# Three row-tile pairs per product through seven block products of sums, in an fp32 encoder trunk

## The chip, the core and the metric

One core of a Trainium2 chip runs the whole program. The metric is device time in microseconds (us) of one execution. The kernel before was run three times: median 2261.09 us, from 2259.49 to 2262.24 us. A separate profiled execution took 2260.93 us, of which 2259.0 us lie between its first and its last instruction (the span).

## What is computed

Two layers of an encoder on 256 tokens with 2048 features, in fp32. Layer 0 mixes tokens by a neighbourhood attention, layer 1 by a short gated convolution; each is followed by a gated MLP of inner width 5632 with a convolution of three taps. Cut to what matters here:

```python
def short_conv_mixer(x, w_in, conv_w, w_out):
    gb, gc, h = jnp.split(x @ w_in, 3, axis=-1)
    return (gb * dwconv_centered(gc * h, conv_w)) @ w_out

def conv_glu_ffn(x, w_up, conv_w, conv_b, w_down):
    h = dwconv_centered(x @ w_up, conv_w) + conv_b
    g, u = jnp.split(h, 2, axis=-1)
    return (jax.nn.silu(g) * u) @ w_down

for i in range(DEPTH):                       # DEPTH = 2
    h = h + mixer(rms_norm(h, mix_norm[i]))  # 0: attention, 1: short convolution
    h = h + conv_glu_ffn(rms_norm(h, ffn_norm[i]), ...)
return rms_norm(h, final_norm)
```

The products `@ w_down` and `@ w_out` of the short convolution are what the change touches.

## The kernel before, in words

**Two kinds of product stage.** A `Phase` (lines 108 to 131) computes features by tokens: for each feature tile of 128 it runs over the K tiles, and each K tile takes two matmuls, line 130 with 512 columns (the weight's high part against the high and low part of the activations side by side) and line 131 with 256 columns (the weight's low part against the high part). A `Tokens` stage (lines 236 to 263) computes tokens by features: the activations are the stationary operand, a block of 512 weight columns the moving one, and the result is to be added to the residual stream `h`, which lies in SBUF as 2 token tiles by 2048 features. For each K tile and each of the two token tiles it runs three matmuls of 512 columns: high by high (line 259), high by low (260), low by high (261). Splitting each fp32 operand into a high and a low part of the faster type keeps the accuracy.

**Tokens stages.** There are six: the attention's output product (16 K tiles), two halves of the down projection in each layer (22 K tiles each) and the short convolution's output (16 K tiles). In each, four column groups g of 512 features are done one after another, each with two PSUM banks of the ring `mm` (four banks); when a group is through, `residual` (line 209) adds both banks to `h`. Where a norm follows (`to_norm`), the group's squares are summed on ScalarE (line 213), and one chunk later its four feature tiles are transposed on TensorE (line 221) and scaled and split into the next stage's input tiles `a` (lines 159 and 160). A Phase behind a norm begins with the first eight K tiles of three feature tiles (`intro=3`), so that input tiles 8 to 15 are needed only from its fourth chunk on. After the last group the norm's factor is worked out (`token_rstd`, lines 224 to 234). `last_evac` does the same for the end of the program and writes the output.

**Weights.** They come in chunks of 128 by 1024 values (512 KB), in a Tokens stage two K tiles of one column group. `prep_to` (lines 89 to 106) issues the chunk's DMA on the SP queue into a tile of the ring `raw` (5 tiles), casts it to its high part on ScalarE (line 97 or 104) and subtracts for the low part on VectorE (98 or 105), into rings `hi` and `lo` of 6 tiles each.

**Order.** The list `items` holds the chunks in the order in which TensorE consumes them. The main loop at the end of `trunk` calls, for each item, `prep_to(c + 1 + AHEAD)` with AHEAD = 4, then the item's `run`, then whatever `after(n, fn)` has put off by n items. This gives the order of priority; the framework that builds the program sets the order of each engine's queue from it and from what is ready in its own reckoning, so an instruction can stand a little earlier or later than it was written. Each queue is served in its order.

**Evacuations around it.** `up_evac` (419 to 436) and `sc_evac` (399 to 414) turn the PSUM results of a Phase into the K tiles `act[...]` and `yT[...]` that the Tokens stage after it reads, on ScalarE and VectorE; `split` (lines 155 and 156) makes their high and low parts. GpSimd has nothing to do in these stages.

Of the kernel before, what the change touches and what calls it, by code (L numbers as in the profile page):

```python
# [12 lines left out]
F32 = mybir.dt.float32  # L14
# [20 lines left out]


# [10 lines left out]
def trunk(ctx, tc, xT, par, bias, wqk, wv, wo, wsc, wscout, wup, wdown, out):  # L47
# [13 lines left out]
    NPAD = 5  # L61
# [27 lines left out]
    def prep_to(n):  # L89
        while len(prepped) < min(n, len(chunks)):  # L90
            src, w, kinds = chunks[len(prepped)]
            raw = wp.tile([P, CH * P], F32, name="raw", tag="raw", bufs=5)
            hi = wp.tile([P, CH * P], F32R, name="hi", tag="hi", bufs=6)
            lo = wp.tile([P, CH * P], F32R, name="lo", tag="lo", bufs=6)
            if kinds == 1:
                nc.sync.dma_start(out=raw[:, :w], in_=src)
                nc.scalar.copy(out=hi[:, :w], in_=raw[:, :w])  # L97
                nc.vector.tensor_sub(out=lo[:, :w], in0=raw[:, :w], in1=hi[:, :w].bitcast(F32))  # L98
            else:

                nc.sync.dma_start(out=raw.rearrange("p (f c) -> p f c", f=4), in_=src.rearrange("f p c -> p f c"))
                r = raw.rearrange("p (f k c) -> p f k c", f=4, c=P)
                hv, lv = (x.rearrange("p (k f c) -> p f k c", f=4, c=P) for x in (hi, lo))
                nc.scalar.copy(out=hv, in_=r)  # L104
                nc.vector.tensor_sub(out=lv, in0=r, in1=hv.bitcast(F32))  # L105
            prepped.append((hi, lo))

    class Phase:
# [3 lines left out]
        def __init__(self, w, fts, nk, src, evac, intro=0, step=CH):  # L112
# [4 lines left out]
            for ft, k0, n in order:  # L117
                k1 = min(k0 + n, nk)
                items.append((self, ft, len(chunks), k0, k0, k1))
                chunks.append((w[ft, :, k0 * P:k1 * P], (k1 - k0) * P, 1))  # L120

        def run(self, ft, c, k0, ka, kb):
            hi, lo = prepped[c]
# [82 lines left out]
    def residual(g, ps):  # L206
        for t in range(2):
            x = h[:, t, g * 4 * P:(g + 1) * 4 * P]
            nc.vector.tensor_add(out=x, in0=ps[t], in1=x)

    def squares(g, ssq):
        for t in range(2):
            nc.scalar.activation(tp.tile([P, 4 * P], F32, name="s", tag="s"), h[:, t, g * 4 * P:(g + 1) * 4 * P],
                                 AF.Square, accum_out=ssq[:, t, g:g + 1])
# [21 lines left out]
    class Tokens:  # L236


        def __init__(self, parts, src, evac):

            self.src, self.evac = src, evac
            self.nk = sum(n for _, n in parts)
            for g in range(KT // 4):
                for i, (w, n) in enumerate(parts):
                    base = sum(m for _, m in parts[:i])
                    for k0 in range(0, n, 2):
                        items.append((self, g, len(chunks), base + k0, base + k0, base + k0 + 2))
                        chunks.append((w[4 * g:4 * g + 4, :, k0 * P:(k0 + 2) * P], 8 * P, 2))

        def run(self, g, c, k0, ka, kb):  # L250
            hi, lo = prepped[c]
            if ka == 0:
                self.ps = [pm.tile([P, 4 * P], F32, name="mm", tag="mm") for _ in range(2)]
            for k in range(ka, kb):
                x = self.src[k]
                wh, wl = (w[:, (k - k0) * 4 * P:(k - k0 + 1) * 4 * P] for w in (hi, lo))
                for t in range(2):
                    xh, xl = (x[:, i + t * P:i + (t + 1) * P] for i in (0, S))
                    nc.tensor.matmul(self.ps[t], lhsT=xh, rhs=wh, start=k == 0, stop=False)  # L259
                    nc.tensor.matmul(self.ps[t], lhsT=xh, rhs=wl, start=False, stop=False)  # L260
                    nc.tensor.matmul(self.ps[t], lhsT=xl, rhs=wh, start=False, stop=k == self.nk - 1)  # L261
            if kb == self.nk:
                self.evac(g, self.ps)

    def to_norm(n, a):
# [3 lines left out]
        def evac(g, ps):  # L269
            residual(g, ps)  # L270
            squares(g, ssq)

            def next_input():
                for k0, tag in ((4 * g, "tr"), (4 * g + 2, "o")):
# [4 lines left out]
            after(1, next_input)  # L279
            if g == KT // 4 - 1:  # L280
                after(2, lambda: nc.vector.tensor_copy(rstd, token_rstd(ssq)))
# [11 lines left out]
    def qk_evac(f, ps):  # L293
# [4 lines left out]
        x["qk"[which]] = tp.tile([P, 2 * S], F32R, name=f"qk{which}", tag=f"qk{which}")  # L298
# [62 lines left out]
    class Values:  # L361


        def __init__(self, g, src):
            self.g, self.src = g, src
            for k0 in range(0, KT, 2):
                items.append((self, g, len(chunks), k0, k0, k0 + 2))
                chunks.append((wv[g, :, k0 * 4 * P:(k0 + 2) * 4 * P], 8 * P, 1))

        def run(self, g, c, k0, ka, kb):  # L370
            hi, lo = prepped[c]
# [13 lines left out]
            for t in range(2):  # L385
                vh = tp.tile([P, 4 * P], F32R, name=f"vh{t}", tag=f"vh{t}", bufs=1)
                vl = tp.tile([P, 4 * P], F32R, name=f"vl{t}", tag=f"vl{t}", bufs=1)
# [8 lines left out]
    yT = [None] * KT  # L396
    sc_of = {}

    def sc_evac(f, ps):
# [11 lines left out]
        else:  # L411
            nc.vector.tensor_mul(out=t, in0=t, in1=sc_of["c"])
            yT[j] = act_tile()
            split(yT[j], t)

# [3 lines left out]
    def up_evac(layer, act):  # L419
        def evac(f, ps):  # L420
# [11 lines left out]
            else:  # L432
                nc.vector.tensor_mul(out=c, in0=c, in1=glu["g"])
                act[j % HALF] = act_tile()
                split(act[j % HALF], c)
        return evac


    def last_evac():
# [3 lines left out]
        def evac(g, ps):  # L443
            residual(g, ps)
            squares(g, ssq)

            def outputs():
                for k0, tag in ((4 * g, "tr"), (4 * g + 2, "o")):
                    tr = transposed(k0, tag)
                    y[k0 // 2] = a_tile().bitcast(F32)  # L450
                    for k in range(2):
                        nc.scalar.activation(y[k0 // 2][:, k * S:(k + 1) * S], tr[:, k, :], AF.Copy,
# [147 lines left out]
```

## Time and profile before

| what | value |
|---|---|
| median of three runs | 2261.09 us |
| profiled execution | 2260.93 us |
| its span | 2259.0 us |
| TensorE matmul, busy | 2235.0 us (99%), 11908 instructions |
| weight load, busy | 1914.8 us (85%) |
| VectorE, busy | 1559.8 us (69%) |
| ScalarE, busy | 1158.4 us (51%) |
| mean granted TensorE clock | 0.997 of full speed |

Busy time is the time in which at least one instruction of the engine was under way. Instructions of one engine overlap a little, so a group's mean duration is longer than the step from one instruction to the next; the step is read from a timeline. For TensorE above all, a matmul's duration is about twice the time by which it moves the end.

### The profile page before, as it was taken

How to read it: one execution, taken by the hardware profiler on the slowest of the kernel's cores; microseconds unless marked ns; L12 is line 12 of the kernel's file. 1: busy time of each engine (PE TensorE's matmuls, PEld its weight loads, DVE VectorE, ACT ScalarE, POOL GpSimd, SP SyncE). 2: the span in 40 equal slices, each digit the busy share in tenths (PEclk: the TensorE clock that was granted, in tenths of full speed). 3: DMA queues.
4: the chain of work that ended last, by engine and by line, in shares of the span. 5: the costliest groups of instructions: out<-in, count | busy, mean ns of one | idle time of the engine just before them, and what ended most of it. 6: DMA issues, size and time to landing. Idle time of an engine off the chain costs nothing.

```text
span 2259.0 us, 31368 instructions
## 1 busy us (share of the span) xinstructions
PE 2235.0 (99%) x11908; PEld 1914.8 (85%) x11908; DVE 1559.8 (69%) x2263; ACT 1158.4 (51%) x1745; POOL 46.7 (2%) x52
## 2 busy tenths in 40 slices
PE   8999999999999999999999999999999999999997
PEld 6888888888888888888888888888888888888886
DVE  7777665688874577776567676558888547777643
ACT  5555545555553455554444444446555435555542
POOL 3110000000000000000000000000000000000000
PEclk9999999999999999999999999999999999999999
DMA  7565555555566655566655555555556665555662
GB/s 239 177 187 176 180 172 189 182 194 187 190 190 192 194 186 187 187 186 187 189 187 192 188 193 188 188 185 188 192 189 188 195 193 189 186 187 187 186 187 93
DMA packets 209687, 420.97 MB, mean 186 GB/s; under 512 B 13312, under 2 KB 136192, under 8 KB 209536
## 3 DMA queue, kind: packets, MB, share of 16 engines
q1 hardware_dynamic: 207792, 414.72, 58.6%
q0 software_dynamic: 1024, 3.15, 0.5%
q8 instruction: 94, 1.54, 0.3%
q10 hardware_dynamic: 720, 1.09, 0.1%
q14 instruction: 57, 0.47, 0.1%
HBM read 416.81 MB, written 2.10 MB: 185 GB/s over the span
## 4 chain that ended last, share of the span: by engine, by line
PE 98%; DVE 1%; issue 0%; ACT 0%; DVEq 0%; ACTq 0%
PE mm L130 42%; PE mm L131 21%; PE mm L261 10%; PE mm L259 10%; PE mm L260 10%; PE mm L379 1%; PE mm L380 1%; PE mm L381 1%; PE tr L221 1%; PE tr L341 0%; DVE a L464 0%; PE o L355 0%; PE o L353 0%; PE sc L316 0%; PE o L354 0%
## 5 line engine op out<-in xcount | busy, mean ns | idle before, releaser
L130 PE MATMUL mm<-a,hi 128*128 128x512 f32 x4096 | 1438.1, 397 | 6.0 <-DVE a L160 4.2
L131 PE MATMUL mm<-a,lo 128*128 128x256 f32 x4096 | 1142.3, 279 | 1.0 <-DVE lo L98 1.0
L130 PEld LDWEIGHTS mm<-a,hi 128*128 128x128 f32 x4096 | 769.2, 188 | 190.8 <-DVE a L160 6.0
L97 ACT CAST hi<-raw 128x1024 fp32r<-128x1024 f32 (+1 forms) x550 | 572.3, 1041 | 652.7 <-issue 516.9
L98 DVE TENSOR_TENSOR lo<-raw,hi 128x1024 fp32r<-128x1024 f32 (+1 forms) x550 | 672.7, 1224 | 335.0 <-ACT hi L97 334.5
L131 PEld LDWEIGHTS mm<-a,lo 128*128 128x128 f32 x4096 | 771.7, 188 | 2.9 <-DVE lo L98 1.9
L105 DVE TENSOR_TENSOR lo<-raw,hi 128x1024 fp32r<-128x1024 f32 x240 | 294.1, 1225 | 286.5 <-ACT hi L104 285.9
L104 ACT CAST hi<-raw 128x1024 fp32r<-128x1024 f32 x240 | 252.8, 1053 | 341.3 <-PE mm L261 266.9
L259 PE MATMUL mm<-hi,act 128*128 128x512 f32 x960 | 374.6, 390 | 0.0
L261 PE MATMUL mm<-hi,act 128*128 128x512 f32 x960 | 373.7, 389 | 0.0
L260 PE MATMUL mm<-lo,act 128*128 128x512 f32 x960 | 373.6, 389 | 0.0
L261 PEld LDWEIGHTS mm<-hi,act 128*128 128x128 f32 x960 | 180.2, 188 | 37.5
L259 PEld LDWEIGHTS mm<-hi,act 128*128 128x128 f32 x960 | 180.2, 188 | 37.0
L260 PEld LDWEIGHTS mm<-lo,act 128*128 128x128 f32 x960 | 180.2, 188 | 36.9
L184 DVE SCALAR_TENSOR_TENSOR conv<-pad,pt,conv 128x256 f32<-128x256 f32 x384 | 185.1, 482 | 8.6 <-ACT conv L182 2.0
L173 DVE TENSOR_TENSOR corr<-mm,corr 128x256 f32<-128x256 f32 x256 | 106.7, 417 | 0.0
L182 ACT ACTIVATE conv<-pad,pt 128x256 f32<-128x256 f32 x176 | 105.2, 598 | 0.8 <-DVE pad L174 0.8
L172 ACT COPY corr<-mm 128x256 f32<-128x256 f32 x256 | 92.7, 363 | 0.1
L174 DVE TENSOR_TENSOR pad<-corr,rstd 128x256 f32<-128x256 f32 x176 | 75.1, 427 | 5.8
L379 PE MATMUL mm<-hi,a 128*128 128x512 f32 x128 | 50.7, 396 | 0.0
L380 PE MATMUL mm<-lo,a 128*128 128x512 f32 x128 | 49.9, 390 | 0.0
L381 PE MATMUL mm<-hi,a 128*128 128x512 f32 x128 | 49.9, 390 | 0.0
(98 smaller groups left out, 793.8 us busy)
## 6 DMA issues: line engine op xcount, KB each, us to landing
raw<-in_wup SPq DMA_DIRECT2D x352, 512.0 KB, 3.6
raw<-in_wdown SPq DMA_DIRECT2D x176, 512.0 KB, 3.8
raw<-in_wsc SPq DMA_DIRECT2D x96, 512.0 KB, 3.6
raw<-in_wqk SPq DMA_DIRECT2D x58, 512.0 KB, 3.8
raw<-in_wv SPq DMA_DIRECT2D x32, 512.0 KB, 4.1
raw<-in_wo SPq DMA_DIRECT2D x32, 512.0 KB, 3.5
raw<-in_wscout SPq DMA_DIRECT2D x32, 512.0 KB, 3.6
raw<-in_wqk SPq DMA_DIRECT2D x12, 256.0 KB, 5.1
```

The source lines that it names most:

```text
L97: nc.scalar.copy(out=hi[:, :w], in_=raw[:, :w])
L98: nc.vector.tensor_sub(out=lo[:, :w], in0=raw[:, :w], in1=hi[:, :w].bitcast(F32))
L104: nc.scalar.copy(out=hv, in_=r)
L105: nc.vector.tensor_sub(out=lv, in0=r, in1=hv.bitcast(F32))
L130: nc.tensor.matmul(ps, lhsT=hi[:, o:o + P], rhs=x, start=k == 0, stop=False)
L131: nc.tensor.matmul(ps[:, S:], lhsT=lo[:, o:o + P], rhs=x[:, :S], start=False, stop=k == self.nk - 1)
L173: nc.vector.tensor_add(out=corr, in0=ps[:, :S], in1=corr)
L182: nc.scalar.activation(c, x[:, 1:S + 1], AF.Identity, scale=w[1], bias=b)
L184: nc.vector.scalar_tensor_tensor(out=c, in0=x[:, tap:tap + S], scalar=w[tap], in1=c, op0=ALU.mult, op1=ALU.add)
L259: nc.tensor.matmul(self.ps[t], lhsT=xh, rhs=wh, start=k == 0, stop=False)
L260: nc.tensor.matmul(self.ps[t], lhsT=xh, rhs=wl, start=False, stop=False)
L261: nc.tensor.matmul(self.ps[t], lhsT=xl, rhs=wh, start=False, stop=k == self.nk - 1)
```

## The change

A pair of K tiles and a pair of column groups form a product of 2 by 2 blocks: two token tiles by two K tiles, times two K tiles by two column groups of 512. Written out it has eight block products. The change computes it, for some pairs, with the scheme of seven block products of sums and differences (Winograd's form of Strassen's algorithm). The pairs are numbers 2, 5 and 8 of the eleven of each down stage (`S_DOWN`), and 1, 3 and 5 of the eight of the short convolution's output (`S_OUT`). The attention's output product has none, but goes through the new loop too.

- A Tokens stage now takes two column groups at a time (g runs over two, not four), with all four `mm` banks, named 11, 21, 12, 22. An item is still one chunk (left or right column group), and both halves of a plain pair are separate items. A pair of the set is one item, `seven`.
- Weights of such a pair: `sums` makes two tiles of sums on VectorE (four additions of 128 by 512), one in the ring `raw`, one in a tile `t24`. Three splits follow for the right chunk, where there was one: half of the raw chunk, and both sums. The left chunk is split as before.
- Activations: `make_forms`, called from the evacuations of the stage before, makes four sums of 128 by 128 on GpSimd, and splits them with one ScalarE copy and one VectorE subtraction of 128 by 512.
- Products: four of the seven accumulate in the PSUM banks of the pool `pa` (`st`, `sc`, `tr`, `o`), three go straight into 11, 12 and 21. One item after the last pair of the set, `combine` adds the four banks to `h`: one ScalarE copy, eight VectorE additions of 128 by 512.
- `residual` and `squares` work on one token tile and column group at a time. Norm inputs are made from two column groups at once (8 feature tiles, four transposing steps on four banks). At the end of the program half of the output scalings move from ScalarE to VectorE.
- To make room, `NPAD` goes from 5 to 3, and a few temporary tiles share tags (`vv`, `qk`).

```diff
+S_DOWN = (2, 5, 8)
+S_OUT = (1, 3, 5)
...
-    NPAD = 5
+    NPAD = 3
...
+            if kind == "cols":
+                prepped.append(parts(r) + (raw,))
             else:
...
+                prepped.append(sums(prepped[-1][2].rearrange("p (f k c) -> p f k c", f=4, c=P), r))
...
+    def sums(l, r):
+
+        t13 = wp.tile([P, CH * P], F32, name="raw", tag="raw", bufs=5)
+        t24 = tp.tile([P, CH * P], F32, name="t24", tag="qk")
+        v13, v24 = (x.rearrange("p (k f c) -> p f k c", f=4, c=P) for x in (t13, t24))
+        add = nc.vector.tensor_add
+        add(out=v13[:, :, 0, :], in0=l[:, :, 0, :], in1=r[:, :, 0, :])
+        add(out=v13[:, :, 1, :], in0=r[:, :, 1, :], in1=r[:, :, 0, :])
+        add(out=v24[:, :, 0, :], in0=v13[:, :, 0, :], in1=r[:, :, 1, :])
+        add(out=v24[:, :, 1, :], in0=v24[:, :, 0, :], in1=l[:, :, 1, :])
+        return parts(r[:, :, 1:2, :]), parts(t13), parts(t24)
...
-            for g in range(KT // 4):
...
+            for g in range(KT // 8):
+                base = 0
+                for w, n in parts:
                     for k0 in range(0, n, 2):
...
+                        k = base + k0
+                        left, right = (w[f:f + 4, :, k0 * P:(k0 + 2) * P] for f in (8 * g, 8 * g + 4))
+                        c = len(chunks)
+                        chunks.append((left, 8 * P, "cols"))
+                        if k // 2 in sset:
+                            chunks.append((right, 8 * P, "sums"))
+                            items.append((self, g, c + 1, k, k, k + 2))
+                        else:
+                            chunks.append((right, 8 * P, "cols"))
+                            items.append((self, g, c, k, k, k + 2))
+                            items.append((self, g, c + 1, k, k, k + 2))
+                    base += n
...
+    def seven(self, g, c, k0):
...
+        if first:
+            self.u = [pa.tile([P, 4 * P], F32, name="mu", tag=n) for n in ("st", "sc", "tr", "o")]
+        a, e, f, b = self.u
+        left, (w22, t13, t24) = prepped[c - 1], prepped[c]
...
+        for ps, x, w, j in ((a, raw(0, 0), left, 0), (self.c["11"], raw(1, 0), left, 1), (self.c["12"], s4, w22, 0),
+                            (e, s1, t13, 0), (f, s3, t13, 1), (b, s2, t24, 0), (self.c["21"], raw(1, 1), t24, 1)):
+            own = ps in self.u
+            self.product(ps, *x, *(y[:, j * 4 * P:(j + 1) * 4 * P] for y in w[:2]), own and first, own and last)
+        if last:
+            after(1, lambda: self.combine(g))
...
+    def combine(self, g):
+
+        a, e, f, b = self.u
+        sa, u = (tp.tile([P, 4 * P], F32, name="s", tag="s") for _ in range(2))
+        o = {(t, n): h[:, t, (2 * g + n) * 4 * P:(2 * g + n + 1) * 4 * P] for t in range(2) for n in range(2)}
+        nc.scalar.copy(out=sa, in_=a)
+        nc.vector.tensor_add(out=u, in0=b, in1=sa)
+        nc.vector.tensor_add(out=o[0, 0], in0=o[0, 0], in1=sa)
+        nc.vector.tensor_sub(out=sa, in0=e, in1=u)
+        nc.vector.tensor_sub(out=o[1, 1], in0=o[1, 1], in1=f)
+        nc.vector.tensor_add(out=u, in0=f, in1=u)
+        nc.vector.tensor_add(out=o[0, 1], in0=o[0, 1], in1=sa)
+        nc.vector.tensor_add(out=o[1, 1], in0=o[1, 1], in1=sa)
+        nc.vector.tensor_add(out=o[1, 0], in0=o[1, 0], in1=u)
...
+    def make_forms(xe, xo):
...
+        nc.gpsimd.tensor_sub(out=v[:, 0, :], in0=x21, in1=x22)
+        nc.gpsimd.tensor_sub(out=v[:, 1, :], in0=v[:, 0, :], in1=x11)
+        nc.gpsimd.tensor_add(out=v[:, 2, :], in0=x12, in1=v[:, 1, :])
+        nc.gpsimd.tensor_sub(out=v[:, 3, :], in0=x11, in1=x21)
+        v = v.rearrange("p f c -> p (f c)")
+        nc.scalar.copy(out=y[:, :4 * P], in_=v)
+        nc.vector.tensor_sub(out=y[:, 4 * P:], in0=v, in1=y[:, :4 * P].bitcast(F32))
+        return y
...
+                for k0, tag in zip(range(4 * q - 4, 4 * q + 4, 2), ("tr", "o", "sc", "st")):
...
+            if t and q % 2:
+                after(1, next_input)
...
+            Tokens([(wdown[layer, half], HALF)], act, evac if half else residual, S_DOWN, forms)
...
+    Tokens([(wscout, KT)], yT, to_norm(3, a3), S_OUT, yforms)
```

## Rows read from the trace of the kernel before

**Rows 1.** The page: engines' busy time; the last chain by engine.

```profile
PE 2235.0 (99%) x11908; PEld 1914.8 (85%) x11908; DVE 1559.8 (69%) x2263; ACT 1158.4 (51%) x1745; POOL 46.7 (2%) x52
...
PE 98%; DVE 1%; issue 0%; ACT 0%; DVEq 0%; ACTq 0%
```

**Rows 2.** The page's groups: weight preparation of token stages.

```profile
L105 DVE TENSOR_TENSOR lo<-raw,hi 128x1024 fp32r<-128x1024 f32 x240 | 294.1, 1225 | 286.5 <-ACT hi L104 285.9
L104 ACT CAST hi<-raw 128x1024 fp32r<-128x1024 f32 x240 | 252.8, 1053 | 341.3 <-PE mm L261 266.9
```

**Rows 3.** Line 259, first down half: min/median/max ns, first and last start.

```profile
L259 PEld LDWEIGHTS mm<-hi,act x176: 187/188/188, 658.5 to 777.4; 128*128 128x128 f32 x176
L259 PE MATMUL mm<-hi,act x176: 389/389/397, 658.6 to 777.6; 128*128 128x512 f32 x176
```

**Rows 4.** Waits: total us, times, longest.

```profile
DVE lo L105 <- ACT hi L104: 285.9, 235, 2.4
ACT hi L104 <- PE mm L261: 266.9, 162, 1.7
```

**Rows 5.** Groups by shape, like the added operations: busy, mean ns.

```profile
L98 DVE TENSOR_TENSOR lo<-raw,hi 128x1024 fp32r<-128x1024 f32 x538 | 664.5, 1235 | 331.6 <-ACT hi L97 331.0
...
L209 DVE TENSOR_TENSOR h<-mm,h 128x512 f32<-128x512 f32 x48 | 30.8, 682 | 13.3 <-PE mm L261 13.3
...
L303 POOL TENSOR_TENSOR bias<-bias,pt 128x384 f32<-128x384 f32 x16 | 22.6, 1413 | 34.0 <-DMA bias<-in_bias 30.2 <-DMA pt<-in_par 3.6
L160 DVE SCALAR_TENSOR_TENSOR a<-tr,pt,a 128x256 fp32r<-128x256 f32 x48 | 22.0, 478 | 5.4 <-ACT a L159 5.4
...
L160 DVE SCALAR_TENSOR_TENSOR a<-act,pt,a 128x256 fp32r<-128x256 f32 x16 | 13.6, 883 | 3.7 <-ACT a L159 3.7
...
L503 POOL TENSOR_TENSOR act<-act 128x512 f32<-128x512 f32 x8 | 10.8, 1347 | 13.2 <-DMA act<-in_xT 13.2
...
L98 DVE TENSOR_TENSOR lo<-raw,hi 128x512 fp32r<-128x512 f32 x12 | 8.2, 725 | 3.4 <-ACT hi L97 3.4
...
L511 DVE TENSOR_TENSOR act<-act 128x512 f32<-128x512 f32 x3 | 2.0, 683 | 0.1
```

**Rows 6.** Timeline of VectorE before a norm: start, us, operation.

```profile
1148.05 1.23 DVE L98 TENSOR_TENSOR lo<-raw,hi 128x1024 fp32r<-128x1024 f32 x1 [1.50 <-ACT hi L97]
1149.20 1.28 DVE L209 TENSOR_TENSOR h<-mm,h 128x512 f32<-128x512 f32 x2
```

**Rows 7.** Windows of three stages: VectorE busy (count), clock, DMA.

```profile
658.50:778.30 119.80, 60.76 (x59) 1.00 0.67 193
1030.00:1153.00 123.00, 65.95 (x71) 1.00 0.66 188
1419.00:1510.50 91.50, 51.80 (x62) 1.00 0.58 187
```

**Rows 8.** Window, one up projection: PE, PEld, DVE, ACT, POOL busy.

```profile
417.00:658.00 241.00, 241.00 (x1391) 210.66 (x1391) 193.95 (x310) 140.23 (x221) 0.00 (x0) 1.00 0.59 189
```

**Rows 9.** The chain in order of time, around one norm.

```profile
1152.46 0.87 PE tr L221 x8
1156.17 0.43 PE st L233 x2
```

**Rows 10.** Timeline of VectorE there: the last input tile.

```profile
1158.36 0.48 DVE L160 SCALAR_TENSOR_TENSOR a<-tr,pt,a 128x256 fp32r<-128x256 f32 x1
```

**Rows 11.** The chain at the program's end.

```profile
2242.76 0.70 DVE h L209
...
2244.22 0.72 ACT s L213 x2
2244.95 1.46 ACT a L452 x4
2246.42 1.28 ACT L191
...
2250.53 0.69 DVE a L464
```

More of the change, by code (lines that the diff above doesn't have):

```diff
@@ L90, in prep_to @@
         while len(prepped) < min(n, len(chunks)):
-            src, w, kinds = chunks[len(prepped)]
+            src, w, kind = chunks[len(prepped)]
             raw = wp.tile([P, CH * P], F32, name="raw", tag="raw", bufs=5)
-            hi = wp.tile([P, CH * P], F32R, name="hi", tag="hi", bufs=6)
-            lo = wp.tile([P, CH * P], F32R, name="lo", tag="lo", bufs=6)
-            if kinds == 1:
+            if kind == "rows":
                 nc.sync.dma_start(out=raw[:, :w], in_=src)
-                nc.scalar.copy(out=hi[:, :w], in_=raw[:, :w])
-                nc.vector.tensor_sub(out=lo[:, :w], in0=raw[:, :w], in1=hi[:, :w].bitcast(F32))
-            else:
[L101 to L105, printed above, removed]
@@ new lines, in parts @@
+    def parts(r):
+        hi = wp.tile([P, CH * P], F32R, name="hi", tag="hi", bufs=6)
+        lo = wp.tile([P, CH * P], F32R, name="lo", tag="lo", bufs=6)
+        if len(r.shape) == 4:
+            hv, lv = (x[:, :4 * r.shape[2] * P].rearrange("p (k f c) -> p f k c", f=4, c=P) for x in (hi, lo))
+        else:
+            hv, lv = (x[:, :r.shape[1]] for x in (hi, lo))
+        nc.scalar.copy(out=hv, in_=r)
+        nc.vector.tensor_sub(out=lv, in0=r, in1=hv.bitcast(F32))
+        return hi, lo
@@ L204, in stats, with residual, squares @@
         rsqrt(rstd, v, rt[:, 0, :], rt[:, 1, :], ps)
[L206 to L214, printed above, removed]
+    def residual(t, q, ps):
+        x = h[:, t, q * 4 * P:(q + 1) * 4 * P]
+        nc.vector.tensor_add(out=x, in0=ps, in1=x)
+    def squares(t, q, ssq):
+        nc.scalar.activation(tp.tile([P, 4 * P], F32, name="s", tag="s"), h[:, t, q * 4 * P:(q + 1) * 4 * P],
+                             AF.Square, accum_out=ssq[:, t, q:q + 1])
     def transposed(k0, tag):
@@ new lines, in __init__ @@
+                    base += n
+        def run(self, g, c, k0, ka, kb):
+            if k0 // 2 in self.sset:
+                return self.seven(g, c, k0)
+            hi, lo, _ = prepped[c]
+            right = len(prepped[c - 1]) == 3 and (self, g, c - 1, k0, ka, kb) in items[at[0] - 1:at[0]]
+            if not right and ka == 0:
+                self.c = {n: pm.tile([P, 4 * P], F32, name="mm", tag="mm") for n in ("11", "21", "12", "22")}
+                self.begun = set()
+            for t in range(2):
+                ps = self.c["12"[t] + "12"[right]]
+                for k in range(ka, kb):
+                    x = self.src[k]
+                    wh, wl = (w[:, (k - k0) * 4 * P:(k - k0 + 1) * 4 * P] for w in (hi, lo))
+                    xh, xl = (x[:, i + t * P:i + (t + 1) * P] for i in (0, S))
+                    self.product(ps, xh, xl, wh, wl, k == 0, k == self.nk - 1)
+                if kb == self.nk:
+                    self.evac(t, 2 * g + right, ps)
@@ L441, in last_evac, with evac @@
         y = [None] * (KT // 2)
-        def evac(g, ps):
-            residual(g, ps)
-            squares(g, ssq)
+        def evac(t, q, ps):
+            residual(t, q, ps)
+            squares(t, q, ssq)
             def outputs():
-                for k0, tag in ((4 * g, "tr"), (4 * g + 2, "o")):
+                for k0, tag in zip(range(4 * q - 4, 4 * q + 4, 2), ("tr", "o", "sc", "st")):
                     tr = transposed(k0, tag)
```

100 lines of the change are left out of this document (57 added, 43 removed).

## The prediction

> **What bounds the kernel now.** I read the page first. TensorE is busy for 99% of the span and makes 98% of the chain that ended last; VectorE is busy for 69%, and hardly stands in the chain [rows 1]. A busy time of 99% says little by itself, because a matmul's duration covers its neighbours, so the next views ask who waits for whom. In a token stage each chunk of weights costs ScalarE a cast of 1.05 us and VectorE a subtraction of 1.23 us [rows 2]. In the first down half, line 259 starts 176 times from 658.6 to 777.6 us, once in three matmuls, with no row that waits: 119.0/175 = 0.680 us for three, 0.2267 us for one [rows 3]. The weight loads in the same rows take 0.188 us each and have room. So a chunk of 12 matmuls takes 2.72 us, against 1.05 and 1.23 us of preparation. And the preparation waits for TensorE, not the other way round: the cast stands still 266.9 us in all until matmuls give a buffer back, and VectorE 285.9 us for the cast [rows 4]. TensorE's matmul count sets the time.
>
> **What is removed.** A pair of the set takes 7 x 3 = 21 matmuls of 512 columns where it took 8 x 3 = 24. There are 3 such pairs in each of 2 column-group pairs, in each of 5 stages (4 down halves, 1 convolution output): 30 pairs, 90 matmuls with their 90 loads. All have the shape and the bank changes of today's, so each is worth the step of rows 3: 90 x 0.2267 = 20.40 us, all on the path. Here a rule of the Trainium skill speaks against the size. The row shows 0.2267 us for each matmul. The page "TensorE: Matmul & The Clock Gate", section "Back-to-back issue gap", gives about 131 ns as the sustained spacing at 512 columns when loads and matmuls are pipelined; by it 90 matmuls would be worth 11.8 us, an estimate from that page. The rows are of this very loop, and I keep 20.40.
>
> **What is added, and its cover.** A VectorE operation on 512 columns takes 0.68 us, the half split 0.73, a 1024 split 1.23 [rows 5]; one behind another they step by 0.60 (1.28 - 0.68) and 1.15 us (1149.20 - 1148.05) [rows 6]. I carry both: steps/durations.
> - Preparation of a set pair: 4 additions, a half split and two full ones where one full one was: 4.15/4.68 us more; 6 of them in a stage, 24.9/28.1 us.
> - `combine`: 8 additions, twice in a stage: 9.6/10.9 us.
> - Sum for a stage: 34.5/39.0 us more of VectorE.
>
> Against the windows [rows 7]: the first down half has 60.76 of 119.80 us; it becomes 95.3/99.8 of 115.7 (18 matmuls, 4.08 us, shorter). The second half goes from 65.95 to 100.5/105.0 of 118.9. The convolution's output is the tight one: 51.80, less four input tiles of 0.48 us that now come behind the stage (1.9), plus the sum: 84.4/88.9 of 87.4. So VectorE stays under TensorE in the down halves, and is level with it there.
>
> Order matters beside the load. Six tiles hold split weights; a chunk could be ready 5 chunks ahead, 13.6 - 1.05 - 1.23 = 11.3 us. A set pair takes four of the six. The tightest chunk is then the one behind it: its tile is given back one chunk (2.72) and one set pair (21 x 0.2267 = 4.76) before it is needed, and 2.28 us of that are its preparation: 5.2 us are left. `combine` (4.8/5.5 us at a stretch) stands behind the last set pair of a group; the chunks behind it use buffers that this pair gave back, and are needed only four chunks later (4 x 2.72 = 10.9 us). I cost both at nothing; the cover is this cushion, and without it each microsecond that VectorE is late is TensorE's.
>
> ScalarE gains a half and a full cast for each set pair (about 1.6 us) and one copy for each `combine`; it has 1.05 us in each 2.72, nothing is lost. The DMAs are the same transfers; the sums hold one more of five raw tiles, and the engines' share of 0.58 to 0.67 leaves room: nothing.
>
> **Forms.** Three times in each stage before, GpSimd does four operations of 128 columns, ScalarE one copy, VectorE one subtraction of 0.68 us. GpSimd's price for 128 columns isn't in the trace: 384 columns took 1.41 us and 512 took 1.35 [rows 5], so 0 to 1.41 each. VectorE may also be slowed meanwhile: the input scaling took 0.88 us at the start, where GpSimd ran, and 0.48 later [rows 5]. If VectorE stood still for all of it, 3 x (4 x 1.41 + 0.68) = 19 us, against 241 - 194 = 47 us that it idles in an up projection [rows 8]. Cost nothing; bounds 0 and 0, as long as that idle time lasts.
>
> **Moved steps.** Where the convolution's output goes from its first to its second half, the right-hand residuals (1.28 us for both) stand on VectorE near the sums of pair 1 of the next half, and TensorE's transposes one item later wait for them. Bounds 0 and two preparations of 4.68; I take one residual pair late, 1.28 us. In the down halves the set starts one pair later: nothing.
>
> At the three norms in the middle, 8 input tiles instead of 4 are made at the end. Before, one Phase chunk took 1156.17 - 1153.33 = 2.84 us, so the token stage ended at 1149.62 [rows 9], and the last tile was ready at 1158.84, 9.2 us later [rows 10]. Four more tiles of 0.48 make 11.1. They are needed after 3 chunks and 1.74 us of transposes, from 10.3 us (tile 8) to 12.8 (tile 15). Nothing, with 1.7 us to spare; the bound is 1.9 us a norm, 5.7 in all.
>
> At the end the chain is residual, squares, four scalings (1.46 us), a table load (1.28 us), the factor, the output multiplications [rows 11]. Four more scalings go to VectorE, where the wait for the table load covers them; the early `Sqrt` is free to run far ahead as before, so the load stays. Nothing; bounds -0.7 (one residual earlier) and +1.5. The smaller `NPAD` and the shared tags wait for readers several evacuations back: nothing.
>
> **Sum.** Profiled execution 2260.93 - 20.40 + 1.28 = 2241.8 us. That execution stands 0.16 us under the median of 2261.09, so no correction. A measurement of this kernel can tell about 0.2%, 4.5 us, from no change.
>
> **Rivals.**
> - A, the forecast: 2241.8.
> - B, VectorE becomes the bound in the convolution's output. For: 84.4/88.9 of 87.4 us, before any waiting of its own. If it waits a tenth of its time for casts, 92.8/97.8, 5.4 to 10.4 over; less the cushion of 5.2, up to 5.2 us: 2247.0. Against: it can start sums as soon as the raw chunks lie there.
> - C, slower: the four additions read runs of 128 out of chunks of another order, and cost more than the 0.68 us of a plain one. Each stage has 24. The output then loses 1.5 us plus 24 times the excess, a down half what goes beyond its 15.9 or 13.9 us of room. At 1.31 us the 19.1 us are gone; at 1.40 the loss is 18.8 + 2 x 1.4 + 2 x 3.4 = 28.4 and the time 2270.2. Against: the split of line 105 reads and writes in just that order, and takes 1.23 us like line 98, which doesn't [rows 2, 5].
> - D, a removed matmul gives back less than its step, since neighbours close up only to the load's pace: 90 x 0.188 = 16.9, so 2245.3. The rule cited above is of this kind; by its figure it would be 2250.4. Rows 3 speak against it.
> - E, the matmuls aren't fewer in effect: 2260.9. The loop's counts speak against it.
>
> **How the numbers follow.** A 0.72, B 0.15, C 0.08, D 0.03, E 0.02. Faster takes A, B and D: 0.90. C lies close to no change at its lower prices (0.03), with E 0.05; its rest is slower, 0.05. The range starts at 2239.0 (no wait, the end 0.7 shorter, and the runs' own spread), and ends at 2249.0, which is B with one norm late by 1.9. It leaves out C, E and the tails of A and B, some 0.15.
>
> **What would show it.** Right: 90 matmuls fewer; lines of the token loop still stepping by 0.227 us; VectorE near 100 us in each down half and near full in the convolution's output; matmul waits for VectorE of a few us in all, most of them at that stage. B shows as waits of the seven's matmuls for the sums there. C shows as a mean of the additions above 1.3 us. D shows as a longer step. Wrong altogether: TensorE idle for more than 0.5 us at each set pair.

## The result, and the profile after

The kernel after took 2247.97 us (median of four runs, 2247.64 to 2251.99), the kernel before beside it 2260.41: a ratio of 0.9948, 95% interval 0.9931 to 0.9965. That is 12.4 us faster, 2.8 times the 0.2% that can be told from no change. The direction was right and the median lies in the range (one of the four runs, 2251.99, doesn't), but 6.2 us above the forecast of 2241.8. The profiled execution took 2248.17 us, so its trace may stand for the rest.

The page after, against [rows 1]: 90 matmuls fewer, as counted, and TensorE still makes 98% of the chain.

```profile
PE 2226.4 (99%) x11818; PEld 1902.9 (85%) x11818; DVE 1740.8 (77%) x2546; ACT 1216.9 (54%) x1822; POOL 85.0 (4%) x110
...
PE 98%; DVE 1%; issue 0%; ACT 0%; DVEq 0%
```

The busy time can't say where the missing 6 us went: TensorE is busy for 99% of both spans. The way to find them is to lay the two traces side by side. Line 259 before and line 304 after begin each K tile's matmuls in a token stage, so their first and last starts are marks that both kernels have. In the first down half, against [rows 3] (columns: durations in ns, then first and last start):

```profile
L304 PE MATMUL mm<-hi,act x140: 389/389/398, 663.5 to 779.1; 128*128 128x512 f32 x140
L304 PE MATMUL mu<-hi,sf x18: 392/392/396, 676.5 to 767.5; 128*128 128x512 f32 x18
L304 PE MATMUL mu<-hi,act x6: 389/389/389, 674.4 to 764.1; 128*128 128x512 f32 x6
L304 PE MATMUL mm<-hi,sf x6: 404/404/404, 675.8 to 765.4; 128*128 128x512 f32 x6
```

The stage ran from 658.6 to 777.6 us before (119.0 us), and from 663.5 to 779.1 after (115.6 us). It is shorter, but it starts 4.9 us later. The same view of every token stage gives the table. A stretch between two token stages is a Phase with its norm.

| stretch of the program | before, us | after, us | change |
|---|---|---|---|
| up to the attention's output | 320.4 | 320.7 | +0.3 |
| attention's output (no sevens) | 92.1 | 91.1 | -1.0 |
| layer 0, first up projection | 246.1 | 251.7 | **+5.6** |
| first down half | 119.0 | 115.6 | -3.4 |
| second up projection | 249.4 | 249.5 | +0.1 |
| second down half | 121.8 | 117.6 | -4.2 |
| short convolution's input | 268.3 | 269.5 | +1.2 |
| short convolution's output | 89.1 | 84.8 | -4.3 |
| layer 1, first up projection | 246.2 | 247.2 | +1.0 |
| first down half | 119.0 | 115.7 | -3.3 |
| second up projection | 249.4 | 249.4 | 0.0 |
| second down half | 121.8 | 117.4 | -4.4 |
| to the end of the span | 16.4 | 16.2 | -0.2 |

In the four stages with a norm or the program's end behind them, one batch of eight transposes (0.87 us in [rows 9]) has moved from inside the stage to behind it. Allowing for that, the attention's output gained 0.1 us, and each stage with sevens 3.3 to 3.5 us, 16.9 in all, where the forecast had 4.08 each and 20.40 in all. With the same allowance, 4.7 us were lost in layer 0's first up projection, in which nothing was changed.

**No wait explains either.** The waits of TensorE after (engine, line waited for: us, times, longest) hold no product of a token stage:

```profile
PE st L257 <- DVE conv L255: 3.8, 1, 3.8
PE mm L156 <- DVE a L186: 3.2, 5, 1.3
PE mm L156 <- ACT hi L118: 1.2, 2, 0.9
```

VectorE carries the added load, though less of it than forecast. Windows of the first two down halves and of the convolution's output (length, VectorE busy with its count, clock, DMA), against [rows 7]:

```profile
663.50:780.00 116.50, 90.92 (x107) 1.00 0.65 200
1028.60:1147.00 118.40, 94.52 (x115) 1.00 0.64 199
1415.60:1502.00 86.40, 78.18 (x99) 1.00 0.61 196
```

VectorE is busy for 90% of the output stage, and still no matmul there waits for a sum.

**What the slow up projection looks like.** Its pairs of matmuls, lines 130 and 131 before, 156 and 157 after, come at another step. The first of each pair, in the same stretch of both kernels; before:

```profile
L130 PE MATMUL mm<-a,hi x535: 392/395/395, 469.7 to 654.8; 128*128 128x512 f32 x179
```

After:

```profile
L156 PE MATMUL mm<-a,hi x524: 395/398/403, 469.9 to 654.7; 128*128 128x512 f32 x175
```

Before, 534 steps in 185.1 us are 0.3466 us a pair; after, 523 steps in 184.8 us are 0.3533. About 700 pairs at 6.7 ns more make 4.7 us: the loss. The median duration, 395 against 398 ns, is the quick way to tell them apart. The kernel before has both steps as well: in this trace 0.3466 in the three Phases behind a norm, 0.353 in both second up projections. So neither step is new; the change moved one Phase from the shorter to the longer.

One difference stands at the start of that Phase, in the order. Behind the norm, the matmul that spreads the norm's factor (line 233 before, 257 after) stands in a stream of pairs. Timeline before (start, us, operation):

```profile
419.55 0.28 PE L131 MATMUL mm<-a,lo 128*128 128x256 f32 x1
419.67 0.60 PE L233 MATMUL st<-conv,ones 128*128 128x256 f32 x2
419.91 0.58 PE L130 MATMUL mm<-a,hi 128*128 128x512 f32 x1
```

After:

```profile
425.58 0.50 PE L156 MATMUL mm<-a,hi 128*128 128x512 f32 x1
425.92 0.28 PE L157 MATMUL mm<-a,lo 128*128 128x256 f32 x1
426.03 0.63 PE L156 MATMUL mm<-a,hi 128*128 128x512 f32 x2
426.50 0.39 PE L157 MATMUL mm<-a,lo 128*128 128x256 f32 x2
...
427.31 0.59 PE L257 MATMUL st<-conv,ones 128*128 128x256 f32 x2
427.55 0.58 PE L156 MATMUL mm<-a,hi 128*128 128x512 f32 x1
```

Before, it stands behind a whole pair; after, two 512s come together and then two 256s, among small waits for input tiles, and it stands between the two halves of a pair. That this order is the cause is at this point only a guess; what the other traces say of it stands behind experiment 9.

### The profile page after: what moved, and what is told of

Its sections match the earlier page's. It is cut to its first block, busy times and chain, and to the rows that moved or that the text cites. A ratio compares the mean times of both kernels' runs of the same rounds, so it can differ in the third digit from the quotient of the medians.

```text
span 2246.4 us, 31725 instructions
## 1 busy us (share of the span) xinstructions
PE 2226.4 (99%) x11818; PEld 1902.9 (85%) x11818; DVE 1740.8 (77%) x2546; ACT 1216.9 (54%) x1822; POOL 85.0 (4%) x110
## 4 chain that ended last, share of the span: by engine, by line
PE 98%; DVE 1%; issue 0%; ACT 0%; DVEq 0%
PE mm L156 42%; PE mm L157 21%; PE mm L304 8%; PE mm L306 8%; PE mm L305 8%; PE mm L474 1%; PE mm L475 1%; PE mm L476 1%; PE mu L305 1%; PE mu L304 1%; PE mu L306 1%; PE tr L245 1%; PE tr L436 0%; DVE a L573 0%; PE sc L412 0%
## 5 line engine op out<-in xcount | busy, mean ns | idle before, releaser
L119 DVE TENSOR_TENSOR lo<-raw,hi 128x1024 fp32r<-128x1024 f32 (+1 forms) x820 | 988.8, 1213 | 392.6 <-ACT hi L118 388.7
L118 ACT CAST hi<-raw 128x1024 fp32r<-128x1024 f32 (+1 forms) x820 | 840.3, 1029 | 825.2 <-issue 465.0
L304 PE MATMUL mm<-hi,act 128*128 128x512 f32 x780 | 304.6, 391 | 0.0
L306 PE MATMUL mm<-hi,act 128*128 128x512 f32 x780 | 304.1, 390 | 0.0
L305 PE MATMUL mm<-lo,act 128*128 128x512 f32 x780 | 303.5, 389 | 0.0
L306 PEld LDWEIGHTS mm<-hi,act 128*128 128x128 f32 x780 | 146.4, 188 | 31.3
L305 PEld LDWEIGHTS mm<-lo,act 128*128 128x128 f32 x780 | 146.5, 188 | 30.5
L304 PEld LDWEIGHTS mm<-hi,act 128*128 128x128 f32 x780 | 146.4, 188 | 30.4
L119 DVE TENSOR_TENSOR lo<-t,hi 128x1024 fp32r<-128x1024 f32 x30 | 36.7, 1224 | 22.9 <-ACT hi L118 22.8
L474 PE MATMUL mm<-hi,a 128*128 128x512 f32 x128 | 50.7, 396 | 0.0
L118 ACT CAST hi<-t 128x1024 fp32r<-128x1024 f32 x30 | 31.5, 1049 | 35.3 <-PE mm L306 32.3
```

Of the source, the lines that this page charges most:

```text
L304: nc.tensor.matmul(ps, lhsT=xh, rhs=wh, start=start, stop=False)
L305: nc.tensor.matmul(ps, lhsT=xh, rhs=wl, start=False, stop=False)
L306: nc.tensor.matmul(ps, lhsT=xl, rhs=wh, start=False, stop=stop)
```

## The experiments

Two questions were open: what set the step of the up projection, and what each stage with sevens lost. Theory 1: the rearranged token loop, which makes eight input tiles at a time, changes the order at a norm, and the Phase behind it then keeps the longer step; the sevens have no part in it. Theory 2, its rival: the rearranged loop by itself costs nothing, and the sevens bring the loss with them. Some expectations name a rival of their own (the second theory of 2 to 4 and theory 3 of experiment 5: the place of the tiles, or work beside TensorE). Theories 4 and 5 are about the sevens' own step and are told where they are tried. Ratios are to runs of the kernel before on the same chip.

**1. The new loop without sevens.**

```diff
-S_DOWN = (2, 5, 8)
-S_OUT = (1, 3, 5)
+S_DOWN = ()
+S_OUT = ()
```

> The changed kernel with both sets empty: every pair of every token stage goes through its eight block products, but with the new loop (two column groups at a time, norm inputs by eight tiles). Theory 1: the missing microseconds come from the rearranged loop (the first up projection runs at the slower of two steps, 0.3535 instead of 0.347 us for a pair of matmuls, as its start is arranged otherwise): the run keeps that and loses the sevens' gain of 3.4 us in each of 5 stages, so about 2248 + 17 = 2265 us, and the first up projection is as slow as in the changed kernel. Theory 2: they come from the sevens themselves (forms on GpSimd, sums on VectorE): the run is then level with the kernel before, 2260.5 us, with the first up projection at 0.347 us for a pair.

Measured: 2268.55 us (2266.61 to 2274.13), ratio 1.004 (1.0026 to 1.0054). Theory 2 falls: without sevens the change is 8 us slower than the kernel before. The smaller `NPAD`, the shared tags and the moved scalings are still in this version, so it doesn't yet single out the loop; experiment 5 does. In the profiled run, the longest (2274.13), the down halves are as before (663.2 to 782.3 us, 119.1), while layer 0's first up projection is on the longer step, 524 steps in 185.2 us:

```profile
L156 PE MATMUL mm<-a,hi x525: 395/398/403, 469.6 to 654.8; 128*128 128x512 f32 x175
```

So are the other two Phases behind norms in that run. The times of its four runs lie up to 7.5 us apart, which suggests that the step of a Phase differs between runs of one program; only one run of each program was traced, so it isn't shown.

**2 to 4. Breaking the stream.** If the step depends on how a stream begins, a foreign matmul in its middle (a break) might change it. One more fp32 matmul of 256 columns (the trace lists it as two), whose result nobody reads, was put in: after the twelfth chunk of layer 0's first up projection (e2); also after the sixth of both second up projections and in three groups of the attention (e3); and in the kernel before, in the second up projections and the attention alone (e4).

```diff
+    def kick(x):
+        st = pa.tile([P, S], F32, name="kick", tag="st")
+        nc.tensor.matmul(st, lhsT=ones, rhs=x, start=True, stop=True)
...
+        if i in kicks:
+            kick(seen[base[0] + kicks[i]])
```

> The changed kernel with one more fp32 matmul (ones by a 128x256 tile, result not used) between two chunks of layer 0's first up projection, behind its twelfth chunk. Theory 1 (the step of a Phase is one of two patterns that stay once entered, and a foreign matmul between two chunks sets the quicker one): from there on 0.347 us for a pair instead of 0.3535, some 600 pairs, 4.0 us less, 0.4 us for the matmul: about 2244.4 us. Theory 2 (the step hangs on where the tiles lie, or on what GpSimd and VectorE do beside it): no change of step, 2248.4 us.

> The same matmul also in the second up projection of each layer (behind the sixth chunk) and in the attention's groups 1 to 3 (behind the fourth chunk): all the Phases that run at the slower step. Theory 1: 4.0 us less in each of the two up projections, 0.2 us in each attention group: about 2235.8 us, quicker than both kernels. Theory 2: six matmuls more, about 2250.5 us.

> The kernel before with the same matmul in the second up projection of each layer and in the attention's groups 1 to 3 (its first up projections run at the quicker step already). Theory 1: 2260.4 - 8.6 = about 2251.8 us: the step has nothing to do with the change. Theory 2: 2262.5 us.

Measured: e2 2246.88 us (2242.46 to 2248.41), ratio 0.9936 (0.9924 to 0.9949); e3 2250.86 (2249.05 to 2254.48), 0.9962 (0.9949 to 0.9974); e4 2253.74 (2253.14 to 2254.70), 0.9971 (0.996 to 0.9983).

In e4 the break worked. The second up projection of layer 0 behind the break; before:

```profile
L130 PE MATMUL mm<-a,hi x502: 395/398/403, 849.7 to 1026.7; 128*128 128x512 f32 x168
```

In e4, where the line has number 139:

```profile
L139 PE MATMUL mm<-a,hi x501: 392/395/395, 849.9 to 1023.2; 128*128 128x512 f32 x167
```

501 steps in 177.0 us against 500 in 173.3: 0.3533 and 0.3466. So the step has nothing to do with sevens, can be changed by one matmul, and is worth some 4 us for each up projection; e4 is the kernel before with 6.8 us less. But in the profiled runs of e2 and e3 the same break changed nothing: in e2 the first up projection stays at 395/398/403 ns, and in e3 both second up projections stay and the short convolution's input falls to the longer step too. e2's median lies between the two times it was to tell apart, and e3 missed by 15 us. A break can change the step, but can't be counted on to.

**5. The old loop at the attention's output alone.** The attention's output product has no sevens; here it goes again through the loop of before (four groups, input tiles by fours), and all else is the kernel after.

```diff
-    Tokens([(wo, KT)], oT, to_norm(1, a1))
+    Tokens4(wo, oT, 1, a1)
...
+    class Tokens4:
...
+                after(1, lambda: self.next_input(g))
...
+            for k0, tag in ((4 * g, "tr"), (4 * g + 2, "o")):
```

> The changed kernel, but the attention's output product (which has no sevens) goes through the old loop again: four column groups one after another, four input tiles made after each. The norm's broadcast matmul then stands between two whole chunks of the first up projection again, as in the kernel before, and not in a stretch whose matmuls are out of their usual order. Theory 1 (the start of a Phase decides which of two steps it keeps, 0.3467 or 0.3533 us for a pair): the first up projection runs at 0.3467, 4.6 us less, about 2243.4 us. Theory 3 (the slow step there comes from where the tiles lie now, or from work beside it): it stays at 0.3533, 2248 us.

Measured: 2242.81 us (four of five runs from 2242.54 to 2243.76, one at 2248.96), ratio 0.9926 (0.9913 to 0.9938). What theory 1 forecast came: 5.2 us come back, and the Phase behind that norm is on the shorter step again, 534 in 185.1 us:

```profile
L156 PE MATMUL mm<-a,hi x535: 392/395/395, 469.8 to 654.9; 128*128 128x512 f32 x179
```

So the new loop at this one boundary brings the longer step. All twelve traces agree: the five programs with the new loop there have the longer step in this Phase, the seven with the old loop (experiments 7 to 10 among them) the shorter. Work on GpSimd beside it doesn't: the forms are made in this version as well. Whether the order does it, or where the tiles come to lie, this run alone can't say. This version beats both kernels, and lies 1 us from the forecast.

**6 and 7. Where the form tiles keep their low part.** The first rows above show the second loss: matmuls of a seven that have a form as stationary operand last 392 to 404 ns, the others 389. Their starts in one seven (timeline after):

```profile
674.43 0.39 PE L304 MATMUL mu<-hi,act 128*128 128x512 f32 x1
...
675.79 0.40 PE L304 MATMUL mm<-hi,sf 128*128 128x512 f32 x1
676.03 0.40 PE L305 MATMUL mm<-lo,sf 128*128 128x512 f32 x1
676.27 0.39 PE L306 MATMUL mm<-hi,sf 128*128 128x512 f32 x1
676.50 0.39 PE L304 MATMUL mu<-hi,sf 128*128 128x512 f32 x1
...
679.28 0.40 PE L304 MATMUL mm<-hi,act 128*128 128x512 f32 x1
```

The first six, with activations, step by 0.2267 us; the next three by 0.24, 0.24 and 0.23; the 21 together take 4.85 us where 21 x 0.2267 is 4.76. The item behind each seven still steps a little longer. Theory 4: in a form tile the low part lies 512 values behind the high part, in an activation tile 256, and the distance costs. e6 lays the forms out like activations in the kernel after, e7 in that of experiment 5.

```diff
...
-        nc.scalar.copy(out=y[:, :4 * P], in_=v)
-        nc.vector.tensor_sub(out=y[:, 4 * P:], in0=v, in1=y[:, :4 * P].bitcast(F32))
+        v = v.rearrange("p (g c) -> p g c", g=2)
+        yh, yl = (y.rearrange("p (g l c) -> p g l c", g=2, l=2)[:, :, l, :] for l in range(2))
+        nc.scalar.copy(out=yh, in_=v)
+        nc.vector.tensor_sub(out=yl, in0=v, in1=yh.bitcast(F32))
```

> The changed kernel with each form's low part 256 values behind its high part, as in an activation tile, where it stands 512 values behind. In the changed kernel's trace the 360 matmuls whose stationary operand is a form step by 0.2305 to 0.2408 us, the others by 0.227, 2.2 us in all. Theory 4: the distance between high and low part does it; they step by 0.227 then and the run takes 2.2 us less, 2245.8 us. Theory 5: it is where the form tiles lie, or something else; no change, 2248 us.

> Both edits of the two runs before together. Theories 1 and 4: 2241.2 us; theory 1 alone: 2243.4 us; neither: 2248 us.

Measured: e6 2248.09 us, ratio 0.9949 (0.9933 to 0.9964), where the kernel after has 2247.97; e7 2242.99, 0.9925 (0.9913 to 0.9938), where experiment 5 has 2242.81. In e6's first down half the matmuls with forms last 392 and 404 ns as before. Theory 4 falls; e7 repeats experiment 5 to 0.2 us.

**8. Sevens without forms.** In the kernel of experiment 5, the four products with a form take a plain activation tile as stationary operand. The sums of the activations are made, but left out of the result.

```diff
+            s1, s2, s4, s3 = raw(0, 0), raw(0, 1), raw(1, 0), raw(1, 1)
```

> The version with the old loop for the attention's output (2242.8 us), in which the four products of each seven that read a form take a plain activation tile as stationary operand instead (the forms are still made, but not used; the sums of activations are left out of the result). Theory 5a: the slower steps in the seven (0.2305 to 0.241 us against 0.227) come from the form tiles as stationary operands; all 21 matmuls step by 0.227 then, and each of the five stages is 0.6 us shorter, about 2239.7 us. Theory 5b: they come from the moving side (the sums of weights) or from the changes of bank; the steps stay, 2242.8 us.

Measured in one run: 2244.69 us. The total says little, since layer 1's first up projection fell to the longer step in this run (229 matmuls in 40 us instead of 233); it takes 251.7 us where experiment 5 has 247.2. Without these 4.5 us the run would lie 0.5 us from the 2239.7 of theory 5a. The sevens themselves say it. The 21 matmuls of one seven now take 4.76 us, without a longer step among them:

```profile
669.89 0.39 PE L304 MATMUL mu<-hi,act 128*128 128x512 f32 x1
...
671.25 0.39 PE L304 MATMUL mm<-hi,act 128*128 128x512 f32 x1
671.48 0.39 PE L305 MATMUL mm<-lo,act 128*128 128x512 f32 x1
671.70 0.39 PE L306 MATMUL mm<-hi,act 128*128 128x512 f32 x1
...
674.65 0.39 PE L304 MATMUL mm<-hi,act 128*128 128x512 f32 x1
```

And the first down half takes 114.9 us, 659.0 to 773.9, which is 119.0 less 4.1, the forecast's 4.08:

```profile
L304 PE MATMUL mm<-hi,act x146: 389/389/397, 659.0 to 773.9; 128*128 128x512 f32 x146
```

So the loss in the stages comes from form tiles as stationary operands. Why such a load steps longer stays open: the distance was refuted, and the forms' values and the place of their tile in SBUF weren't tried apart.

**9. More breaks.** Four breaks in each second up projection of experiment 5's kernel, 6, 8, 10 and 12 chunks in, to learn whether the step can be chosen.

```diff
+                for m in range(4):
+                    kicks[len(items) + 6 + 2 * m] = m
```

> The version with the old loop for the attention's output, with four foreign matmuls in each second up projection, behind its sixth, eighth, tenth and twelfth chunk. Theory 1, with the addition that a break sets the quicker step by chance and that it then stays: both projections at 0.3467 us for a pair over some 650 pairs, 2 x (4.3 - 1.7) = 5.2 us less, about 2237.6 us, in most runs; 2246.2 us where neither takes it. If the step can't be moved in this program: 2246.2 us in every run.

Measured: 2251.36 us in two heaps (2246.66 to 2247.31, 2255.40 to 2256.14), ratio 0.9956 (0.9941 to 0.9971). It missed: in the profiled run none of the eight breaks changed the step, and two Phases behind norms fell to the longer one. One of them, the short convolution's input (window: TensorE's count in brackets), has 228 matmuls in 40 us where the kernel after has 233:

```profile
1260.00:1300.00 40.00, 40.00 (x228) 34.69 (x228) 29.36 (x43) 18.94 (x27) 2.77 (x4) 1.00 0.58 189
```

**What all traces say of the place at the norm.** In the twelve traces of this case (the two kernels and the ten experiments) the matmul that spreads the norm's factor stands in the stream of a Phase 36 times, three times in each; its place was read from TensorE's order. Seven times it stands between the two halves of a pair, as shown above for the kernel after: in layer 0's first up projection in the kernel after, e1, e2, e3 and e6, in the short convolution's input in e1, and in layer 1's first up projection in e10. Behind all seven the Phase has the longer step. The other 29 times it stands behind a whole pair; then the step is the shorter one 24 times and the longer one 5 times (the short convolution's input in e3 and e9, layer 1's first up projection in e1, e8 and e9). So the guess has the traces on its side, but the order isn't all. In the kernel after and in e3, TensorE's order is the same through the first 400 matmuls of the short convolution's input, and the starts of the 80 ahead of the norm's matmul keep one distance to the nanosecond. Behind it the two part. After:

```profile
1160.02 0.67 PE L257 MATMUL st<-conv,ones 128*128 128x256 f32 x2
...
1160.88 0.40 PE L156 MATMUL mm<-a,hi 128*128 128x512 f32 x1
...
1162.96 0.40 PE L156 MATMUL mm<-a,hi 128*128 128x512 f32 x1
```

In e3, where the lines have numbers 267 and 165:

```profile
1160.81 0.67 PE L267 MATMUL st<-conv,ones 128*128 128x256 f32 x2
...
1161.66 0.40 PE L165 MATMUL mm<-a,hi 128*128 128x512 f32 x1
...
1163.78 0.40 PE L165 MATMUL mm<-a,hi 128*128 128x512 f32 x1
```

Six pairs lie between the last two rows of each: 2.08 us after, 2.12 us in e3. Ahead of the norm's matmul both streams step by 0.3526 us. So the step is set where the foreign matmul stands, not where the Phase begins, and with one and the same order it can come out either way.

**10. How near VectorE's limit is.** In experiment 5's kernel each of the four additions of `sums` is done twice: 24 more operations with a step of 0.60 us in each stage with sevens, 14.4 us.

```diff
         add(out=v13[:, :, 0, :], in0=l[:, :, 0, :], in1=r[:, :, 0, :])
+        add(out=v13[:, :, 0, :], in0=l[:, :, 0, :], in1=r[:, :, 0, :])
```

> The version with the old loop for the attention's output, with each of the four additions of weights done twice: 24 more VectorE additions of 0.60 to 0.68 us in each of the five stages, 14.4 to 16.3 us. VectorE is busy 78.2 of 86.4 us in the convolution's output and 89 to 95 of 116 to 118 us in the down halves of the changed kernel. If the work beside TensorE is hidden only while VectorE has room: nothing in the down halves, and in the convolution's output an excess of 6 to 8 us, of which up to 5.2 are taken by the cushion: 2244 to 2251 us. If VectorE's work has far more room than its busy share says: 2242.8 us. If set pairs wait for the sums already: 15 us and more in every stage, above 2300 us.

Measured: 2257.38 us (2251.06 to 2262.90), ratio 0.9987 (0.9978 to 0.9997), above the 2244 to 2251 that were expected for this case. The first down half holds: VectorE goes from 90.71 to 102.91 us of 117, and TensorE works through. In the convolution's output it doesn't: its marks run from 1410.0 to 1502.5 us (92.5) where experiment 5 has 1410.9 to 1495.7 (84.8). The waits there name the sums, first the cast and then VectorE behind the cast:

```profile
ACT hi L118 <- DVE raw L131: 13.1, 5, 3.8
ACT hi L118 <- DVE t L135: 10.3, 4, 2.9
DVE lo L119 <- ACT hi L118: 9.1, 11, 1.5
```

And TensorE stands idle with VectorE busy throughout (columns: length, busy time with count of PE, PEld, DVE, ACT, POOL, then PE's clock, DMA share and GB/s):

```profile
1450.00:1460.00 10.00, 7.39 (x35) 5.71 (x34) 10.00 (x16) 3.55 (x9) 0.00 (x0) 0.94 0.26 84
```

In these and the next 10 us the granted clock reads 0.94 and 0.89, means over its two levels (1.2 and 2.4 GHz), where the stages of the other runs show 1.00: here a stall went with a lower clock as well. Beyond the 7.7 us of the stage itself, the layer's first up projection behind it, from that stage's last mark to the next one's first, takes 255.2 us where experiment 5 has 247.2: its norm comes late, and it falls to the longer step. This second loss the expectation didn't have. The cover that the forecast named is real in the down halves, and thin in the output stage.

## Why the prediction was right, and where it was off

**What held.** TensorE's matmul count sets the time, and 90 matmuls with their loads left the path. The preparation, `combine` and the forms lie beside TensorE, and no product waits for them; VectorE's share of it was put too high (90.92 us in the first down half, where 95.3 to 99.8 were forecast). Experiment 8 gives the price of a removed matmul as taken: the five stages become 4.1, 3.9, 4.0, 4.0 and 4.1 us shorter (the moved transposes allowed for), 20.1 against 20.40. By the rule of the Trainium skill that was weighed there (page "TensorE: Matmul & The Clock Gate", section "Back-to-back issue gap", 131 ns) it would have been 11.8, an estimate from that page. The trace doesn't agree with it: plain products step by 227 ns in both kernels.

**Term 1, mis-sized: the step of the seven's own matmuls.** "All have the shape and the bank changes of today's" was right, but four of the seven products take a stationary operand from another tile, and experiment 8 shows that this is what costs 0.6 to 0.7 us a stage (against experiment 5). The stages gave 16.9 us instead of 20.40. That equals rival D's figure by chance: D had neighbours closing up only to the load's pace, while the plain matmuls keep 0.2267 us and the loss goes with the forms.

**Term 2, failed: the norms, "Nothing, with 1.7 us to spare".** It asked whether input tiles come late, and small waits for them are there, 3.2 us in the whole program; behind the other two norms, the moved transposes allowed for, the stretch is 0.3 and 0.1 us longer in the table. The price was not the wait but the step behind it: layer 0's first up projection went to the longer step and lost 4.7 us, near the stated bound of 5.7 for all norms, by a mechanism that isn't in the text. Experiment 1 shows that it comes without the sevens, experiment 5 that it comes from the new loop at this one norm.

**Term 3, not there: 1.28 us at the output's middle.** The residuals did come late, but the scheduler had put matmuls between two batches of the transposes, so nothing stood still (timeline of TensorE):

```profile
1460.31 1.25 PE L245 MATMUL tr<-pt,h 128*128 128x128 f32 x10
1461.31 0.48 PE L304 MATMUL mm<-hi,act 128*128 128x512 f32 x1
...
1463.02 0.82 PE L245 MATMUL tr<-pt,h 128*128 128x128 f32 x6
```

The miss in the sum: 4.7 + 3.5 - 1.28, less some 0.5 us in smaller gains (the program's end above all: about 1.1 by the table, once the moved transposes are allowed for), is the 6.4 us between 2248.17 and 2241.8.

**Luck.** That the median still lies in the range is luck in part: its upper end, 2249.0, was worked out from rival B and one late norm, and neither came; losses of about that size came from two places that the text didn't have. Experiment 5 at 1 us from the forecast is luck too: what is left of its misses, 3.5 us lost to the forms against 1.28 that didn't come and about 1.1 gained at the end, nearly cancels.

**The rivals.** B didn't happen: the output stage took 78.18 us of VectorE and not 84.4 or more, and nothing waited. Experiment 10 shows that its mechanism is possible: with 14.4 us more of VectorE's work in the stage it is there. C falls by the mean of the additions, 0.68 to 0.69 us and not 1.31 (groups of VectorE in the output stage: busy us, mean ns):

```profile
L128 DVE TENSOR_TENSOR raw<-raw 128x512 f32<-128x512 f32 x5 | 3.4, 687 | 2.1 <-DMA raw<-in_wscout 2.1
L129 DVE TENSOR_TENSOR raw<-raw 128x512 f32<-128x512 f32 x5 | 3.4, 683 | 0.0
```

E falls by the count. GpSimd's unknown price lay inside its bounds of 0 to 1.41 us, with one operation far dearer than its neighbour:

```profile
L349 POOL TENSOR_TENSOR s<-s,conv 128x128 f32<-128x128 f32 x12 | 15.9, 1322 | 0.9
...
L348 POOL TENSOR_TENSOR s<-conv 128x128 f32<-128x128 f32 x12 | 5.6, 463 | 128.7 <-DVE conv L533 128.7
```

## What to carry to other kernels

Where TensorE is busy all the time, compare the step of its matmuls stage by stage, in the stages that a change doesn't touch as well: a loop rearranged at a boundary can cost a quarter of what the change brings in a stage that it never edits. Cost a removed instruction by the step of what remains, with the operands that remain: the same shape from another tile needn't keep the step. Where a loop is rearranged for some stages, measure the others with the old one: here the attention's output did better without it.

## What was not expected of the hardware

- A long stream of alternating 512- and 256-column matmuls holds one of two steps, 0.3466 or 0.3533 us a pair, for a whole stage without any wait. Which one differs between programs, between Phases of one program, and, as the times suggest, between runs of one program (experiments 5 and 7: four of five runs within 1.3 us, the fifth some 5 us longer; one run of each was traced). One foreign matmul in mid-stream changed it in both second up projections of the kernel before, and in none of those of the kernels after. The norm's own matmul is such a place too: between the halves of a pair the longer step followed 7 times of 7, behind a whole pair 5 times of 29. What decides in the cases of one and the same order stays open.
- Matmuls of one shape stepped by 0.227 us with activation tiles as stationary operand, and by up to 0.24 with form tiles; the cause is open.
- On GpSimd, two subtractions of 128 by 128, one behind the other, took 463 and 1322 ns. The second reads the first one's result; the third operation reads the second's and takes 523, so that alone isn't the reason. It wasn't tried.
